# Two-layer float32 trunk on one core: four chained down accumulators, additions moved to the vector engine, transposes moved ahead

## The chip, the cores and the metric

One core of a Trainium2 chip runs the whole program in one launch. The core has a matrix engine (TensorE, PE in the profile, with PEld for its weight loads), a vector engine (VectorE, DVE), an activation engine (ScalarE, ACT), a general engine (GpSimd, POOL) and a queue that issues the DMAs (SyncE, SP). Each takes its own list of instructions in order, and waits on semaphores where it needs another's result. The matrix engine writes into PSUM (eight banks of 128 x 512 float32); the tiles that the other engines work on lie in SBUF. The metric is the device time of one execution in microseconds (us).

## The reference

The input is 1024 tokens of 1024 channels, and there are two layers. Every sub-layer is wrapped alike:

```
def sandwich(h, g_pre, g_post, fn):
    return x + rmsnorm(fn(rmsnorm(x, g_pre)), g_post)
def swiglu(h, w_gate, w_up, w_down):
    return (jax.nn.silu(h @ w_gate) * (h @ w_up)) @ w_down
```

Layer 0 mixes tokens by differential attention beside a convolution, layer 1 by an S5 state space beside latent attention. Each mixer ends in an output projection of 1024 x 1024; after each stands a SwiGLU of inner width 2816. All is float32, and accurate: each operand is split into a high part that the matrix engine takes in one pass and the remainder, and a product is three passes, high x high, high x low, low x high.

## The kernel before

**The pieces.** `mm3` (L114) issues the three passes. `wsplit` (L1116) makes a weight's high part on ACT and its low part on POOL (L1121). `to_T` transposes 128 rows through the PSUM tag `tr` (two one-bank slots). `sandwich` (L157) finishes 128 rows of a sub-layer: the row load, the sum of squares on ACT (L106), the reciprocal root on POOL (L97, L98), the scaling by root and gain on DVE (L164), the residual addition (L165) on the engine that the caller names, the store, and where a layer follows the next norm (L169).

**The SwiGLU** (`Ffn`) multiplies 2 x 2 blocks with seven products instead of eight (Strassen's scheme in Winograd's form). `x_sums` (L1094) prepares four input sums T1 to T4 and their splits; `up` writes seven forms of the hidden blocks to `h_s` in DRAM. `down` (L1227) goes through the eleven groups of the inner width one and then two at a time. A product (`prod`, L1258) of two groups is 24 matmuls: four blocks of 128 tokens, two groups, three passes; two token blocks share a PSUM tile of two banks (tag `big`, two slots). After half of them DVE adds the tile into an SBUF accumulator (L1229): seven accumulators, one for each product. The hidden blocks are split on ACT (L1248) and DVE (L1249), weight differences are formed on POOL (L1273, `g`). `top` does products 1, 5, 6, 2, 3, `low` does 7 and 4.

**The end of `down`.** For the last two steps (groups 7 to 10) `top` runs first for both. In the last `top` the seven accumulators are combined (`comb`, L1279 to L1282: two sums on POOL and five on DVE, each in two instructions of 128 x 1024). Then `end(0, ...)` runs `sandwich` for token blocks 0 to 3, and products 7 and 4 of the last four groups follow, 48 matmuls each, chained over these groups in PSUM, product 7 added into two accumulators, and `end(1, ...)` runs `sandwich` for blocks 4 to 7. In layer 0 (`end0`, L1412) the transposes of blocks 0 to 3 (`X1[0]`) are issued inside `end(1, ...)`, those of blocks 4 to 7 in `mla_in` (L803), between the first input projections of layer 1.

**Around the output projection.** `w_out_last` (L502) adds the second half of the projection to a stored part (L510), runs `sandwich` with POOL as the residual engine, and transposes the rows of two steps ago by `Ffn.to_T`, whose last difference (L1092) is on POOL. For each token block the projected input is split into one buffer `jt` (L484 on ACT, L485 on DVE).

**The order.** The program is written per tile; a planner (`schedule_with_timeline_sim=True`, L1547) puts the instructions of each engine in order by program order and modelled readiness. What runs is the fixed order it made.

Of the kernel before, what the change touches and what calls it, by code (L numbers as in the profile page):

```python
# [20 lines left out]
P = 128  # L21
# [14 lines left out]
class Trunk:  # L36
# [77 lines left out]
    def mm3(self, ps, a, b, first, last):  # L114
        mm = self.nc.tensor.matmul
# [41 lines left out]
    def sandwich(self, acc, tb, res, hout, gpost, gpre, r, eng):  # L157
# [6 lines left out]
        nc.vector.scalar_tensor_tensor(acc, acc, rs, v3(gpost), op0=ALU.mult, op1=ALU.mult)  # L164
        eng.tensor_tensor(r, r, acc, op=ALU.add)  # L165
# [336 lines left out]
    def w_out_last(self, Y, src, res, hout, gpost, gpre, G, pool, fin=None):  # L502
# [3 lines left out]
        for tb in range(8):  # L506
# [4 lines left out]
            self.sandwich(a, tb, res, hout, gpost, gpre, pool.tile([P, D], F32, tag="nr", name="nr", bufs=2), nc.gpsimd)  # L511
# [291 lines left out]
    def mla_in(self, X, pool, sp, accB, x2a):  # L803
# [59 lines left out]
        for hf in range(2):  # L863
# [21 lines left out]
            if hf == 0:  # L885
                x2a.close()
# [165 lines left out]
class Ffn:  # L1052
# [15 lines left out]
    def to_T(self, xn, tb):  # L1068
# [20 lines left out]
        if t:  # L1089
            v(f1[1], tr, f0[0], op=sub)  # L1090
            v(f1[0], tr, f1[0], op=sub)
            nc.gpsimd.tensor_tensor(f0[1], f0[1], f1[1], op=sub)  # L1092

    def x_sums(self, pool):  # L1094
# [11 lines left out]
        self.T3 = split(t("T3"), F1[:, 0], nc.gpsimd)  # L1106
        self.T4 = split(self.bx.tile([P, 4, 2, HALF], F32R, tag="f", name="T4"), F0[:, 1], nc.gpsimd)
# [119 lines left out]
    def down(self, end, ap, mid=None):  # L1227
        nc, K, v = self.nc, self.K, self.nc.vector
        add = lambda o, a, b: v.tensor_tensor(o, a, b, op=ALU.add)  # L1229
        hs = ExitStack()  # L1230
        hp = hs.enter_context(self.left("hp"))
        acc15 = ap.tile([P, 4, 2, HALF], F32, tag="a15", name="acc15")
        acc6 = ap.tile([P, 4, HALF], F32, tag="a6", name="acc6")
        acc23 = K.yp.tile([P, 4, 2, HALF], F32, tag="y", name="acc23")
        acc47 = K.yp.tile([P, 4, 2, HALF], F32, tag="y", name="acc47")
        a = {1: acc15[:, :, 0], 5: acc15[:, :, 1], 6: acc6, 2: acc23[:, :, 0], 3: acc23[:, :, 1], 4: acc47[:, :, 0], 7: acc47[:, :, 1]}

        half = lambda tag: hp.tile([P, 2, HALF], F32R, tag=tag, name=tag, bufs=3)
        spare = [half("hh"), half("hl")]
# [6 lines left out]
        def hsplit(r, n):  # L1246
            hi, lo = (spare.pop(0), spare.pop(0)) if spare else (half("hh"), half("hl"))
# [4 lines left out]
        def mm(ps, HW, tb, n):  # L1252
# [298 lines left out]
```

## Time and profile before

| what | value |
|---|---|
| median of three runs | 2391.94 us (2391.46 to 2400.63) |
| the profiled execution | 2392.32 us, span 2390.5 us, mean granted TensorE clock 0.955 |
| busy: PE, DVE, POOL, ACT | 2172.1, 1587.8, 1393.1, 952.2 us |
| layer 0: output projection; `up`; `down` | about 440 to 528; 528 to 980; 985 to 1230 us |
| layer 1: mixer; `up`; `down` | about 1245 to 1710; 1710 to 2135; 2136 to 2379 us |

Times in rows count from the start of the span. In a row of the timeline stand the start, the duration, the engine, the line, the operation, what it writes and reads, its shape, and in brackets how long its engine was idle before it and for whom it waited. The granted clock is 1 at 2.4 GHz and 0.5 at 1.2 GHz. A matmul's own duration (some 390 ns) overlaps the next one's; the distance of their starts is the rate.

### The profile page before, as it was taken

Reading aid. Unit: us, or ns where it says so; the run is one execution under the profiler, and the core shown is the slowest. Engines: PE = TensorE matmul, PEld = TensorE weight load, DVE = VectorE, ACT = ScalarE, POOL = GpSimd, SP = SyncE. Lnnn points to the kernel's source line nnn. Section 1 sums busy time; section 2 is a strip of 40 time slices with the busy share of each in tenths; the row PEclk is TensorE's granted clock in tenths of the full one; section 3 lists DMA queues with packets and bytes.
Section 4 is the critical chain, followed back from the end, with each engine's and each line's share of the span. In section 5 each row is a group of like instructions: output and inputs, shape, how many; then the busy total and the mean of one; then the engine's idle time right before and its main releaser. Section 6 shows DMA issues by size and latency. Waiting matters only on the chain. (4 is left out here: it accounts for less than half of the span.)

```text
span 2390.5 us, 27147 instructions
## 1 busy us (share of the span) xinstructions
PE 2172.1 (91%) x9684; PEld 1755.7 (73%) x9684; DVE 1587.8 (66%) x2091; ACT 952.2 (40%) x1419; POOL 1393.1 (58%) x790
## 2 busy tenths in 40 slices
PE   7999889876999999899768888998799999999995
PEld 5887677665888878688656776876688888877874
DVE  6869567679756865677883467756764444448778
ACT  5554555442222232433243346654522222234332
POOL 5997202264665556787843536423775656569786
PEclk9999899988999999999888999999899999999997
DMA  5134663342332333655453375324432323255543
GB/s 206 62 120 146 172 175 102 107 149 69 121 115 97 125 129 106 198 161 163 125 178 104 110 234 154 115 80 148 138 102 93 127 72 132 75 177 163 164 130 132
DMA packets 153735, 315.34 MB, mean 132 GB/s; under 512 B 20224, under 2 KB 43904, under 8 KB 153600
## 3 DMA queue, kind: packets, MB, share of 16 engines
q1 hardware_dynamic: 153600, 313.60, 40.8%
q8 instruction: 77, 1.26, 0.2%
q14 instruction: 58, 0.48, 0.1%
HBM read 214.39 MB, written 96.01 MB: 130 GB/s over the span
## 5 line engine op out<-in xcount | busy, mean ns | idle before, releaser
L1121 POOL TENSOR_TENSOR wl<-raw,wh 128x1024 fp32r<-128x1024 f32 (+1 forms) x238 | 607.4, 2556 | 335.9 <-ACT wh L1119 319.4
L1119 ACT CAST wh<-raw 128x1024 fp32r<-128x1024 f32 (+1 forms) x238 | 242.7, 1023 | 456.8 <-PE b L119 258.9
L118 PE MATMUL b<-T,wh 128*128 128x512 f32 x704 | 277.9, 396 | 16.3 <-DVE F L1170 13.0
L120 PE MATMUL b<-T,wl 128*128 128x512 f32 x704 | 277.4, 394 | 1.1 <-POOL wl L1121 1.1
L119 PE MATMUL b<-T,wh 128*128 128x512 f32 x704 | 277.7, 394 | 0.6 <-DVE T L1100 0.6
L118 PE MATMUL psd<-wh,hh 128*128 128x512 f32 x552 | 222.8, 404 | 37.7 <-DVE acc L1229 26.5
L118 PE MATMUL b<-B,wh 128*128 128x512 f32 x528 | 209.2, 397 | 21.2 <-DVE c L1161 17.6
L119 PE MATMUL psd<-wl,hh 128*128 128x512 f32 x552 | 219.9, 398 | 0.0
L120 PE MATMUL psd<-wh,hl 128*128 128x512 f32 x552 | 219.1, 398 | 0.0
L119 PE MATMUL b<-B,wh 128*128 128x512 f32 x528 | 208.2, 395 | 0.7 <-DVE B L1088 0.7
L120 PE MATMUL b<-B,wl 128*128 128x512 f32 x528 | 207.7, 395 | 0.8 <-POOL wl L1121 0.8
L1229 DVE TENSOR_TENSOR acc<-acc,psd 128x1024 f32<-128x1024 f32 x124 | 150.7, 1217 | 82.7 <-PE psd L120 82.6
L1170 DVE TENSOR_TENSOR p<-p,b 128x1024 f32<-128x1024 f32 (+1 forms) x88 | 83.4, 949 | 144.6 <-PE b L120 134.7
L1248 ACT CAST hh<-hr 128x1024 fp32r<-128x1024 f32 (+1 forms) x84 | 82.4, 981 | 240.0 <-PE psd L119 215.1
L118 PEld LDWEIGHTS b<-T,wh 128*128 128x128 f32 x704 | 133.1, 189 | 47.8 <-issue 13.6
L118 PEld LDWEIGHTS psd<-wh,hh 128*128 128x128 f32 x552 | 106.1, 192 | 70.1 <-issue 27.9
L91 POOL TENSOR_TENSOR wl<-raw,wh 128x1024 fp32r<-128x1024 f32 x48 | 121.6, 2546 | 61.6 <-ACT wh L89 61.4
L120 PEld LDWEIGHTS b<-T,wl 128*128 128x128 f32 x704 | 133.1, 189 | 31.8 <-POOL wl L1121 1.5
L119 PEld LDWEIGHTS b<-T,wh 128*128 128x128 f32 x704 | 133.3, 189 | 31.0 <-DVE T L1100 1.1
L1249 DVE TENSOR_TENSOR hl<-hr,hh 128x1024 fp32r<-128x1024 f32 (+1 forms) x84 | 145.7, 1738 | 11.9 <-ACT hh L1248 11.9
L1273 POOL TENSOR_TENSOR raw<-raw 128x1024 f32<-128x1024 f32 (+1 forms) x50 | 123.4, 2468 | 20.7 <-DMA raw<-in_l_dn_dram 18.3
L1171 DVE TENSOR_TENSOR raw<-raw 128x1024 f32<-128x1024 f32 x66 | 108.3, 1640 | 40.4 <-POOL wl L1121 39.1
(420 smaller groups left out, 5209.2 us busy)
## 6 DMA issues: line engine op xcount, KB each, us to landing
raw<-in_l_gu_dram SPq DMA_DIRECT2D x96, 512.0 KB, 3.5
hr<-l_h_s SPq DMA_DIRECT2D x70, 512.0 KB, 3.9
raw<-in_l_dn_dram SPq DMA_DIRECT2D x48, 512.0 KB, 3.8
l_h_s<-F SPq DMA_DIRECT2D x66, 256.0 KB, 2.2
raw<-in_w_in_dram SPq DMA_DIRECT2D x27, 512.0 KB, 4.0
l_h_s<-c SPq DMA_DIRECT2D x44, 256.0 KB, 2.0
l_h_s<-p SPq DMA_DIRECT2D x44, 256.0 KB, 2.4
raw<-in_l_w_out_dram SPq DMA_DIRECT2D x16, 512.0 KB, 4.1
```

The costliest lines, as they stand in the source:

```text
L91: nc.gpsimd.tensor_tensor(lo, raw, hi.bitcast(F32), op=ALU.subtract)
L118: mm(ps, ah, bh, start=first, stop=False)
L119: mm(ps, ah, bl, start=False, stop=False)
L120: mm(ps, al, bh, start=False, stop=last)
L1119: nc.scalar.copy(hi[:, 0:n], r[:, 0:n])
L1121: nc.gpsimd.tensor_tensor(lo[:, 0:n], r[:, 0:n], hi[:, 0:n].bitcast(F32), op=ALU.subtract)
L1170: add = lambda o, a, b: v.tensor_tensor(o, a, b, op=ALU.add)
L1171: sub = lambda o, a, b: v.tensor_tensor(o, a, b, op=ALU.subtract)
L1229: add = lambda o, a, b: v.tensor_tensor(o, a, b, op=ALU.add)
L1248: nc.scalar.copy(hi[:, 0:n], r[:, 0:n])
L1249: v.tensor_tensor(lo[:, 0:n], r[:, 0:n], hi[:, 0:n].bitcast(F32), op=ALU.subtract)
L1273: g = lambda o, x, y: nc.gpsimd.tensor_tensor(o[:, s], x[:, s], y[:, s], op=ALU.subtract)
```

## The change

- `down` keeps four accumulators. Products 1, 6, 5, 3 run in that order into the same two PSUM tiles without a restart, and after each the running sum is added into one accumulator (`wide`, 8 additions of 128 x 1024). Product 2 runs into four one-bank tiles (`slim`), and so does 7 with 4 chained on it: 12 additions of 128 x 512. The one-bank tiles are tags `tr`, `o` and `f`. All `comb` sums go. The differences for the last products 7 and 4 are formed on DVE (five in the tail); in the loop they stay on POOL.
- `sandwich` gets a second form (`m` given): the gain is multiplied while the root is computed, then one instruction scales and adds. The layer 1 `end1` uses it, on DVE.
- The residual addition of `w_out_last`, the last difference of `Ffn.to_T` and the low parts of T3 and T4 go from POOL to DVE.
- In layer 0 `end0` issues the transposes of blocks 0 to 3 right behind each block's `sandwich`, ahead of products 7 and 4. The tile for them is opened before `down`.

```diff
-            self.sandwich(a, tb, res, hout, gpost, gpre, pool.tile([P, D], F32, tag="nr", name="nr", bufs=2), nc.gpsimd)
+            self.sandwich(a, tb, res, hout, gpost, gpre, pool.tile([P, D], F32, tag="nr", name="nr", bufs=2), nc.vector)
...
+        if m is None:
+            nc.vector.scalar_tensor_tensor(acc, acc, rs, v3(gpost), op0=ALU.mult, op1=ALU.mult)
+            eng.tensor_tensor(r, r, acc, op=ALU.add)
+        else:
+            eng.tensor_tensor(v3(m), acc, v3(gpost), op=ALU.mult)
+            nc.vector.scalar_tensor_tensor(r, v3(m), rs, r, op0=ALU.mult, op1=ALU.add)
...
-            nc.gpsimd.tensor_tensor(f0[1], f0[1], f1[1], op=sub)
+            v(f0[1], f0[1], f1[1], op=sub)
...
-        self.T3 = split(t("T3"), F1[:, 0], nc.gpsimd)
-        self.T4 = split(self.bx.tile([P, 4, 2, HALF], F32R, tag="f", name="T4"), F0[:, 1], nc.gpsimd)
+        self.T3 = split(t("T3"), F1[:, 0], nc.vector)
+        self.T4 = split(self.bx.tile([P, 4, 2, HALF], F32R, tag="f", name="T4"), F0[:, 1], nc.vector)
...
+        def wide(pss, HW, n, k, start=False):
             for tp in range(2):
                 for b in range(2):
+                    mm(pss[tp][:, b], HW, 2 * tp + b, n, start)
+                drain(k, 2 * tp, 2 * tp + 2, pss[tp])
+
+        def slim(pss, HW, n, k, start=True):
+            for tb in range(4):
+                mm(pss[tb], HW, tb, n, start)
+                drain(k, tb, tb + 1, pss[tb])
+
+        def four():
+            return [*self.duo("tr", "psd"), *self.duo("o", "psd")]
+
+        def top(i, n):
+            pss = [K.pp.tile([P, 2, HALF], F32, tag="big", name="psd") for _ in range(2)]
+            B11 = ld(0, i, n)
+            wide(pss, [(hx(0, i, n), self.wsplit(B11, n))], n, (0, 0), True)
+            B12, T = ld(1, i, n), self.raw(None)
+            minus(nc.gpsimd, T, B12, B11, n)
+            W5 = self.wsplit(T, n)
+            B22 = ld(3, i, n)
+            minus(nc.gpsimd, T, B22, T, n)
+            wide(pss, [(hx(5, i, n), self.wsplit(T, n))], n, (1, 0))
+            wide(pss, [(hx(1, i, n), W5)], n, (1, 1))
+            wide(pss, [(hx(4, i, n), self.wsplit(B22, n))], n, (0, 1))
+            B21 = ld(2, i, n)
+            slim(four(), [(hx(2, i, n), self.wsplit(B21, n))], n, (0, 0))
             return B12, B21, B22, T
...
+        top(i1, n)
+        B = top(i2, n)
+        W7 = [w7(B, n, v)]
+        W4 = [w4(B, n, v)]
+        rows = lambda k: [ap.tile([P, D], F32, tag="r", name="r", bufs=4) for _ in range(k)]
+        end(0, out[0], rows(2), 0)
+        C12, C22 = ld(1, i1, n), ld(3, i1, n)
+        minus(v, C12, C22, C12, n)
+        W7.append(self.wsplit(C12, n))
+        q = four()
+        slim(q, [(hx(6, i, n), W) for i, W in zip((i2, i1), W7)], n, (1, 1))
+        end(0, out[0], rows(2), 2)
+        C11, C21 = ld(0, i1, n), ld(2, i1, n)
+        minus(v, C21, C21, C12, n)
+        minus(v, C21, C21, C11, n)
+        W4.append(self.wsplit(C21, n))
+        slim(q, [(hx(3, i, n), W) for i, W in zip((i2, i1), W4)], n, (1, 0), False)
         hs.close()
+        end(1, out[1], rows(4), 0)
...
-            for b in range(4):
-                K.to_T(st[0](b), X1[0], b)
+            X1.append(xb)
         for b, r in enumerate(res, b0):
             K.sandwich(row(b), 4 * hf + b, K.h1, K.h2, *st["g"], r, nc.vector)
+            if hf == 0:
+                K.to_T(row(b), X1[0], b)
```

`drain` adds a PSUM tile into its accumulator on DVE (the first time it copies, on ACT or DVE), `w7` and `w4` form and split a difference on the engine given.

## Rows read from the trace of the kernel before

**Rows 1.** Busy time by stage: window and length, PE, PEld, DVE, ACT, POOL, PEclk, DMA.
```profile
440.00:528.00 88.00, 79.65 (x357) 61.95 (x355) 55.02 (x64) 39.45 (x71) 42.98 (x44) 0.96 0.47 162
985.00:1177.00 192.00, 189.48 (x803) 152.70 (x804) 140.05 (x105) 78.15 (x82) 153.86 (x58) 0.98 0.55 173
1177.00:1275.00 98.00, 59.45 (x230) 45.51 (x229) 81.98 (x63) 35.31 (x57) 51.31 (x44) 0.76 0.44 147
2136.00:2326.50 190.50, 188.69 (x804) 151.01 (x804) 147.20 (x105) 78.72 (x82) 153.52 (x58) 0.99 0.54 172
2326.50:2379.20 52.70, 32.78 (x122) 25.05 (x120) 48.22 (x32) 11.91 (x18) 37.53 (x24) 0.84 0.35 120
488.00:491.20 3.20, 3.20 (x9) 2.55 (x8) 0.41 (x1) 0.89 (x2) 1.40 (x4) 0.52 0.30 120
```

**Rows 2.** Waits of PE, whole span: total us, times, longest us.
```profile
PE psd L118 <- DVE acc L1229: 26.5, 3, 12.3
...
PE ps L118 <- DVE acc L1229: 13.3, 6, 4.5
...
PE b L118 <- DVE F L1170: 13.0, 1, 13.0
...
PE psw L120 <- DVE jt L485: 10.4, 8, 1.7
```

**Rows 3.** Timeline, DVE and PE at the end of down; last row layer 1.
```profile
1175.21 3.40 DVE L1282 TENSOR_TENSOR acc<-acc,acc 128x1024 f32<-128x1024 f32 x1 [1.17 <-POOL acc L1282]
...
1181.82 6.63 DVE L1282 TENSOR_TENSOR acc<-acc,acc 128x1024 f32<-128x1024 f32 x2
...
1188.37 1.21 DVE L1229 TENSOR_TENSOR acc<-acc,psd 128x1024 f32<-128x1024 f32 x1
...
1189.72 0.76 PE L118 MATMUL psd<-wh,hh 128*128 128x512 f32 x1 [12.31 <-DVE acc L1229]
...
2339.08 0.77 PE L118 MATMUL psd<-wh,hh 128*128 128x512 f32 x1 [12.32 <-DVE acc L1229]
```

**Rows 4.** The combining sums on DVE, whole span: count, shortest/median/longest ns, first and last start.
```profile
L1282 DVE TENSOR_TENSOR acc<-acc,acc x20: 1207/2217/3402, 1170.7 to 2352.5; 128x1024 f32<-128x1024 f32 x20
```

**Rows 5.** Next norm of token blocks 4 and 7, timeline of DVE, layer 0.
```profile
1249.41 1.28 DVE L169 SCALAR_TENSOR_TENSOR acc<-acc,rstd,gpre 128x1024 f32<-128x1024 f32 x1 [0.99 <-POOL rstd L98]
...
1273.77 1.29 DVE L169 SCALAR_TENSOR_TENSOR acc<-acc,rstd,gpre 128x1024 f32<-128x1024 f32 x1 [1.27 <-POOL rstd L98]
```

**Rows 6.** The last two vector instructions of the kernel, timeline.
```profile
2383.82 1.28 DVE L164 SCALAR_TENSOR_TENSOR acc<-acc,rstd,gpost 128x1024 f32<-128x1024 f32 x1 [0.72 <-POOL rstd L98]
2385.13 1.23 DVE L165 TENSOR_TENSOR acc<-acc,acc 128x1024 f32<-128x1024 f32 x1
```

**Rows 7.** Timeline of POOL, DVE and PE in layer 0's output projection.
```profile
468.77 0.69 DVE L485 TENSOR_TENSOR jt<-yattn,jt 128x512 fp32r<-128x512 f32 x1
...
484.28 2.38 POOL L165 TENSOR_TENSOR nr<-nr,pa 128x1024 f32<-128x1024 f32 x1 [3.26 <-DVE pa L164]
...
484.72 2.49 DVE L485 TENSOR_TENSOR jt<-yattn,jt 128x512 fp32r<-128x512 f32 x1
...
487.26 0.51 PE L120 MATMUL psw<-wh,jt 128*128 128x512 f32 x1 [1.67 <-DVE jt L485]
```

**Rows 8.** Timeline, the input sums of layer 0's up, DVE and POOL.
```profile
554.27 2.27 DVE L1100 TENSOR_TENSOR T<-F,T 128x2048 fp32r<-128x2048 f32 x1
...
556.47 4.64 DVE L545 SCALAR_TENSOR_TENSOR xd<-xd,xd 128x8 f32<-128x8 f32 x1
...
563.42 4.59 POOL L1100 TENSOR_TENSOR T<-F,T 128x2048 fp32r<-128x2048 f32 x1
...
563.52 4.53 DVE L547 TENSOR_SCALAR xd<-xd 128x8 f32<-128x8 f32 x1
```

**Rows 9.** Groups in 1016 to 1177 us, by form: busy us, mean ns, idle before.
```profile
L1229 DVE TENSOR_TENSOR acc<-acc,psd 128x1024 f32<-128x1024 f32 x57 | 69.5, 1218 | 44.6 <-PE psd L120 44.5
...
L1121 POOL TENSOR_TENSOR wl<-raw,wh 128x1024 fp32r<-128x1024 f32 x29 | 82.5, 2848 | 23.7 <-ACT wh L1119 23.7
```

More of the change, by code (lines that the diff above doesn't have):

```diff
@@ L112, in bcast, with mm3 @@
         return t
-    def mm3(self, ps, a, b, first, last):
-        mm = self.nc.tensor.matmul
+    def mm3(self, ps, a, b, first, last, go=False):
+        mm = lambda *t, **k: self.nc.tensor.matmul(*t, skip_group_check=go, **k)
         ah, al = a
@@ L1225, in up, with down, ld, minus @@
         self.xs.close()
-    def down(self, end, ap, mid=None):
+    def down(self, end, ap):
         nc, K, v = self.nc, self.K, self.nc.vector
-        add = lambda o, a, b: v.tensor_tensor(o, a, b, op=ALU.add)
         hs = ExitStack()
         hp = hs.enter_context(self.left("hp"))
[L1232 to L1236, printed above, removed]
+        out = [K.yp.tile([P, 4, 2, HALF], F32, tag="y", name="acc") for _ in range(2)]
+        C = {(t, c): out[t][:, :, c] for t in range(2) for c in range(2)}
+        seen = set()
         half = lambda tag: hp.tile([P, 2, HALF], F32R, tag=tag, name=tag, bufs=3)
-        spare = [half("hh"), half("hl")]
+        def ld(blk, i, n):
+            return self.raw(self.dn[blk, i:i + n].rearrange("g p c -> p g c"), n)
+        def minus(eng, o, x, y, n):
+            eng.tensor_tensor(o[:, 0:n], x[:, 0:n], y[:, 0:n], op=ALU.subtract)
         def hraw(blk, i, n):
@@ L1255, in mm, with drain @@
                 for g in range(n):
-                    K.mm3(ps, (H[0][:, g, ts], H[1][:, g, ts]), (W[0][:, g], W[1][:, g]), i + g == 0, (i, g) == (len(HW) - 1, n - 1))
-        def prod(k, H, W, n, first):
+                    K.mm3(ps, (H[0][:, g, ts], H[1][:, g, ts]), (W[0][:, g], W[1][:, g]), start and i + g == 0, (i, g) == (len(HW) - 1, n - 1), True)
+        def drain(k, lo, hi, ps):
+            dst = C[k][:, lo:hi] if hi > lo + 1 else C[k][:, lo]
+            if (k, lo) not in seen:
+                seen.update((k, b) for b in range(lo, hi))
+                if lo < 2:
+                    nc.scalar.copy(dst, ps)
+                else:
+                    v.tensor_copy(dst, ps)
+            else:
+                v.tensor_tensor(dst, dst, ps, op=ALU.add)
@@ L1322, in down @@
-        B = top(i2, n, True)
-        free = [t[:, 2 * j:2 * j + 2] for t in (a[1], a[5], a[6], a[1]) for j in range(2)]
-        end(0, acc23, free[0:2], 0)
-        g, hx2, wx, ld = tools(i2, n)
-        _, hx1, _, ld1 = tools(i1, n)
-        B12, B21, B22, T = B
-        g(B12, B22, B12)
-        HW7 = [(hx2(6), wx(B12))]
-        g(B21, B21, T)
-        comb(v, 6, 6, 7)
-        comb(v, 7, 6, 5)
-        comb(v, 4, 4, 6)
-        end(0, acc23, free[2:4], 2)
-        C12, C22 = ld1(1), ld1(3)
@@ new lines, in w7, with w4 @@
+        def w7(B, n, eng):
+            minus(eng, B[0], B[2], B[0], n)
+            return self.wsplit(B[0], n)
+        def w4(B, n, eng):
+            minus(eng, B[1], B[1], B[3], n)
+            return self.wsplit(B[1], n)
+        for i, n in ((0, 1), *((i, 2) for i in range(1, NF // 2 - 4, 2))):
+            B = top(i, n)
+            q = four()
+            slim(q, [(hx(6, i, n), w7(B, n, nc.gpsimd))], n, (1, 1))
+            slim(q, [(hx(3, i, n), w4(B, n, nc.gpsimd))], n, (1, 0), False)
```

98 lines of the change are left out of this document (12 added, 86 removed).

## Prediction

> **What bounds the kernel now.** I read the busy time by stage first. In the body of both `down` stages PE works 189.48 of 192.00 us and 188.69 of 190.50 us at a granted clock of 0.98 and 0.99 [rows 1]. Nothing that leaves PE's own work alone can win there. It is otherwise at the two ends. From 1177 to 1275 us PE is busy 59.45 of 98.00 us, at a mean clock of 0.76; from 2326.5 to 2379.2 us 32.78 of 52.70 us, at 0.84 [rows 1]. DVE is busy 81.98 and 48.22 us there.
>
> The second view is the waits of PE. 26.5 us go to products that wait for the addition L1229, in three waits, and 13.3 us more to the last chained products [rows 2]. The third view, the timeline, shows why an addition of 1.21 us keeps PE waiting for 12.31 us in layer 0 and 12.32 us in layer 1: on DVE it stands behind combining sums, two of which take 6.63 us together [rows 3], where the shortest of the twenty takes 1.207 us [rows 4]. They are stretched: a DVE instruction that reads two SBUF tiles lasts until the POOL instruction beside it is over. The split L485 takes 0.69 us alone, and 2.49 us when it starts 0.44 us after a POOL addition of 2.38 us [rows 7]. The addition out of PSUM kept its 1.21 us [rows 3].
>
> So the ends are bound by what DVE and POOL can do one after the other, and the clock there falls to the lower of its two levels as well: the matmul at 1189.72 lasts 0.76 us [rows 3], against a spacing of 190.50 / 804 = 0.237 us in the body [rows 1].
>
> **The change part by part.** The sum is made against the profiled execution, 2392.32 us (1.8 us around its span of 2390.5); the median of three runs is 2391.94 us, the same within 0.4 us.
>
> *The body of `down`.* The matmuls are as many as before. A full round of two groups had 14 additions of 1.218 us [rows 9], now 8 of these and 12 of half the size; 0.69 us [rows 7] is my price for one. That is 12 x 0.69 - 6 x 1.218 = +1.0 us of DVE per round, beside 38 to 40 us of PE; DVE waited 44.6 us for PE in 161 us [rows 9], which hides it. Reuse of the two wide tiles is as tight as before: PE comes back to a tile after 12 matmuls (2.8 us). The one-bank tiles are four, with 3 x 6 matmuls (4.3 us) between. What is new is that product 6 comes second, so four POOL steps (difference, split, difference, split) must be done before it instead of two. One costs 2.85 us on average [rows 9], 11.4 us for four; the products in front (2, 7, 4 of the round before and 1) last 4 x 24 x 0.237 = 22.8 us. Hidden, with 11 us to spare. Lower bound -3 us (all the body's PE idle time), upper bound +61 us (a rival below); I take +2.
>
> *The end in layer 1.* The combining sums go: per layer ten on DVE and four on POOL. Product 7 is drained once. What stays on DVE and POOL from 2326.5 on, each at its unstretched length and in a row: four weight splits on POOL (2.4 each, as the POOL addition in rows 7: 9.6), four hidden splits and five differences on DVE (9 x 1.21 = 10.9), two instructions for each of the first four token blocks (1.21 + 1.28: 10.0), and four reciprocal roots (about 0.75 each, an estimate from the 0.72 us that DVE waits for one in rows 6 plus their start: 3). Sum 33.5 us. PE needs 120 matmuls x 0.237 = 28.4 us. So the larger, 33.5 us, plus 1 us for the first chain's start, stands against 52.7: -18.2 us. Behind the last product the chain of root, L164 and L165 loses L165, 1.23 us [rows 6], as the gain is multiplied while ACT and POOL make the root: -1.2. Together -19 us. Bounds: PE alone as limit, -24.3 - 1.2 = -25.5; nothing but the final addition, -1.
>
> *The end in layer 0.* The same sum with three DVE instructions a block (1.28 + 1.22 + 1.28, four blocks: 15.1) and two roots each (6): 9.6 + 10.9 + 15.1 + 6 = 41.6 us until product 4 is drained. Then come blocks 4 to 7. Before, their next norms ran from 1249.41 to 1273.77 us, four of them, 8.1 us apart [rows 5], behind the transposes of blocks 0 to 3 on the same engines. These transposes now lie between product 2 and the end of product 4, or just behind it, since two of their PSUM slots hold product 4's first sums: 8 halves of 0.69 us on DVE, 5.5 us, which DVE does from PSUM. I give 41.6 + 8 (the first block's chain) + 3 x 8.1 = 74 us against 98: -24 us. The moved step issues 32 transposes on PE, eight casts on ACT and eight remainders on DVE, no DMA and nothing on POOL; on PE, a transpose that waits for its block holds up the products behind it, which is rival 2. The row loads and stores of `sandwich` keep their place in SP's queue, and the four row tiles are free for blocks 4 to 7 once blocks 0 to 3 are stored, as the reused accumulators were. The tile that is opened earlier pushes the hidden blocks' tiles to other places, so their first loads may wait a little longer or shorter at the start of `down`; that is in the +2 above. Bounds: PE's own work is 59.45 x 0.76 = 45 us, so at best -53; at worst the sum stays DVE's 81.98 us less the ten combining sums at their shortest (12 us) plus five differences (6 us) and a start of 10 us, 86: -12. To lose there it needs the rival below.
>
> *Output projection.* Eight additions a layer go from POOL (2.38) to DVE (1.21). The seven to eight waits of 10.4 us for the split of `jt` [rows 2] come from the POOL addition [rows 7], and after some of them the clock is at the lower level for 3.2 us with 9 matmuls instead of 13 [rows 1]. If the split goes ahead of the addition it ends 1.8 us sooner and the wait is gone; if it goes behind, 0.6 us sooner. So between 8 x 0.6 = 5 and 10.4 + 3 = 13 us less over both layers, were PE's wait all. Against it, DVE has 8 x 1.21 = 9.7 us more per layer beside 55.02 of 88 us [rows 1], which can put off other drains: up to +5. I take -7.
>
> *Input sums.* T3 and T4 took POOL about 4.59 us each and DVE would take 2.27 [rows 8]. In layer 0 tiny DVE instructions stood behind them for 4.64 and 4.53 us [rows 8], in the queue that ends with the 13.0 us wait for L1170 [rows 2]. So DVE's queue is 9.2 - 4.5 = 4.6 us shorter; -4, bounds -9 (both hidden) and +5 (DVE longer and still stretched by other POOL work). In layer 1 PE has no such wait: 0. The difference L1092 (0.7 us on DVE) is hidden behind the same waits.
>
> Sum: 2 - 19 - 24 - 7 - 4 = -52; 2392.3 - 52 = **2340 us**.
>
> **The rivals.**
> 1. *The shared path fills up.* The ends stay bound by DVE and POOL because the vector engine's new differences collide with the weight splits and the early split of the next stage's weights (six of 2.4 us, 14 us) comes into the same row. For: ten sums at 2.2 us median [rows 4] show how stretched it runs. Against: POOL loses 4 x 2.4 + 5 x 2.4 us there. Layer 0 then saves 10, layer 1 9, projection and sums 3, body +2: **2372 us**. The Trainium skill (SBUF — State Buffer, Who interferes with whom) has the rule: GpSimd and a vector instruction with two SBUF inputs lock each other out of a shared port pair for the whole instruction. By that rule moving a difference to the vector engine frees nothing that runs beside it, only the difference of durations; the trace agrees (2.49 against 0.69 us). It would give this rival's time.
> 2. *The transposes don't lie under the products.* Their two PSUM slots are also product 7's and 4's. They then run behind product 4 as before, or hold up product 7 by a block's chain (8 to 10 us). Layer 0 saves 14 instead of 24: **2350 us**.
> 3. *PE becomes the bound at both ends*, with waits of a few us: -45 in layer 0, -23 in layer 1, -13, -8, 0 in the body: **2303 us**. For: PE's own work. Against: the sums of 33.5 and 41.6 us above.
> 4. *Slower: product 6 starves.* If the buffers for its two differences come free only with product 4, the four POOL steps (11.4 us) have only product 1 (5.7 us) in front: 5.7 us a round, five full rounds a layer, 57 us, and as much clock loss as makes 61. The gains fall to it: 2392 - 54 + 61 = **2399 us**. It decides from 5 us a round on. Against: weights have five slots and raw blocks five, and the slots that product 6 of the next round takes are freed by product 2 and the differences, before 7 and 4 run.
> 5. *The clock.* PE now returns to the same two PSUM tiles over four products; if its short pauses there put a tenth of the body at the lower level, that costs 0.1 x 382 = 38 us: **2378 us**. Against: the body cycled through the same two tiles before, at 0.98 and 0.99 [rows 1]. The Trainium skill (TensorE: Matmul & The Clock Gate, A second HAM failure mode: psum-queue depth-cycling) says that cycling through PSUM banks with small pauses makes the clock swing; the body here does not bear that out.
>
> **How the numbers follow.** Forecast 0.50, rivals 0.15, 0.12, 0.12, 0.07 and 0.04. What can be told from no change begins at 0.5%, 12 us. The forecast and rivals 2, 3 and most of 1 and 5 are faster by more: 0.88; the rest of 1, 4 and 5 within 0.5%: 0.06; rival 4: 0.06 slower. The range, 2304 to 2374 us, takes in most of rival 3 and of rival 1 and leaves out 4.
>
> **What would show it.** The two waits of 12.3 us are gone and no wait over 6 us stands at either end; the stretch from the last top's end to the first `psc` is near 74 us in layer 0, and 34 us to PE's end in layer 1; one DVE instruction behind the last root; `jt` waits under 5 us in total; the body still at 0.98 and 0.237 us a matmul. It is wrong if PE waits for L1121 or L1273 in every round, or if new waits for weights at the ends sum to over 15 us a layer.

## The result, and the profile after

The changed kernel takes **2334.07 us** (median of four runs, 2331.67 to 2341.0) against 2391.70 us of the kernel before beside it: a ratio of 0.9754, 95% interval 0.9727 to 0.9782. Forecast were 2340 us. The profiled execution took 2335.67 us, its span is 2333.9 us. PE's busy time went from 2172.1 to 2155.4 us, POOL's from 1393.1 to 1275.4; DVE's stayed (1583.1 us).

The first view answers [rows 1]: the output projection of layer 0, then each `down`, cut in two at the end of its 804th matmul, first layer 0, then layer 1. In the new order these 804 take in the first four products of the last `top`; its fifth, 24 matmuls, already belongs to the end. Where the prediction says "the last top's end", this cut is meant.

```profile
440.00:528.00 88.00, 78.25 (x367) 61.24 (x366) 67.66 (x80) 43.85 (x76) 27.62 (x39) 0.99 0.49 172
969.60:1167.80 198.20, 190.08 (x804) 152.63 (x805) 160.18 (x139) 74.66 (x78) 145.24 (x51) 0.98 0.51 162
1167.80:1235.60 67.80, 52.64 (x211) 41.28 (x210) 52.34 (x44) 29.84 (x47) 34.61 (x34) 0.85 0.47 154
2094.50:2292.20 197.70, 190.35 (x803) 153.20 (x804) 155.57 (x140) 74.79 (x78) 143.37 (x51) 0.98 0.50 162
2292.20:2324.20 32.00, 29.55 (x122) 23.52 (x121) 27.71 (x28) 11.64 (x18) 15.23 (x15) 0.95 0.44 147
```

Both ends are much shorter: 67.8 us where the kernel before needs 96.1 from its 804th matmul to the first `psc`, and 32.0 where [rows 1] has 52.7. PE is busy for 92% of the end in layer 1, so hardly anything but PE is left there. But the two bodies, forecast at +2 us in all, are *longer*: 198.2 and 197.7 us, with PE's busy time nearly what it was.

The second view, PE's longest waits over the whole span (total, times, longest), answers [rows 2].

```profile
PE psd L115 <- ACT hh L1252: 20.3, 2, 12.3
PE psd L115 <- DVE acc L1271: 17.7, 10, 3.0
PE tr L181 <- DVE xt L184: 11.2, 5, 4.7
PE b L115 <- DVE c L1163: 10.4, 3, 5.1
```

The two waits of 12.3 us for an addition behind combining sums are gone. The wait for `F` is 3.1 us instead of 13.0, and those for DVE's half of `jt` come to 0.5 us instead of 10.4; for ACT's half PE waits 6.9 us in the two projections (5.6 before). What leads now are the two waits for the first hidden block at the start of `down`, 12.3 and 8.0 us (5.4 and 4.0 before), and ten short ones for drains. One more row of the kernel before, its second longest, which [rows 2] leaves out and the prediction doesn't use, has come down too:

```profile
PE b L118 <- DVE c L1161: 17.6, 2, 9.1
```

These are waits behind each output projection, 8.5 us in layer 0 and 9.1 in layer 1, for `c`, the additions on DVE that drain the first products of `up`. In the changed kernel they are 4.0 and 6.4 us.

The span cut at PE's own landmarks (first or last matmul of a product, read from both timelines):

| stretch | before | after | difference |
|---|---|---|---|
| start to layer 0's last output projection | 447.1 | 446.5 | -0.6 |
| layer 0: output projection and input sums, to the first product with T1 | 107.4 | 95.7 | -11.7 |
| `up`, to its last product | 424.9 | 414.7 | -10.2 |
| to the first `down` product | 5.8 | 12.7 | +7.0 |
| `down`, to the 804th matmul's end | 192.0 | 198.2 | +6.2 |
| to layer 1's first `psc` | 96.1 | 67.8 | -28.3 |
| layer 1: mixer and output projection | 418.5 | 414.0 | -4.5 |
| to the first product with T1 | 42.2 | 39.2 | -3.0 |
| `up` | 398.0 | 397.4 | -0.6 |
| to the first `down` product | 4.4 | 8.4 | +4.0 |
| `down`, to the 804th matmul's end | 190.2 | 197.7 | +7.5 |
| to PE's end | 52.6 | 32.0 | -20.6 |
| to the end of the span | 11.3 | 9.7 | -1.6 |

The sum is -56.4 us of the spans' -56.6. So the total came near the forecast because misses of both signs met: some 25 us lost at the start of `down` and in its last `top`s, where 2 were forecast, and some 15 us more won ahead of it, 7 at the ends and 4 in layer 1's mixer stretch. The experiments went after these.

### The profile page after: what moved, and what is told of

The parts are those of the page before. It is cut to its first block, busy times and chain, and to the rows that moved or that the text cites. A ratio compares the mean times of both kernels' runs of the same rounds, so it can differ in the third digit from the quotient of the medians.

```text
span 2333.9 us, 27188 instructions
## 1 busy us (share of the span) xinstructions
PE 2155.4 (92%) x9684; PEld 1744.8 (75%) x9684; DVE 1583.1 (68%) x2175; ACT 945.6 (41%) x1413; POOL 1275.4 (55%) x740
## 3 DMA queue, kind: packets, MB, share of 16 engines
q1 hardware_dynamic: 150528, 313.60, 41.6%
## 4 chain that ended last, share of the span: by engine, by line
PE 68%; DVE 13%; DMA 6%; issue 5%; POOL 4%; ACT 3%; SPq 1%; POOLq 0%; DVEq 0%; ACTq 0%
PE b L115 30%; PE psd L115 13%; PE psw L115 6%; PE psc L115 5%; PE psq L115 3%; PE po L115 2%; PE pss L1038 2%; POOL wl L1123 2%; PE trp L365 1%; DVE hl L1253 1%; DVE acc L1271 1%; DMA bm<-k_s 1%; PE psv L115 1%; PE psu L115 1%; DMA hr<-l_h_s 1%
## 5 line engine op out<-in xcount | busy, mean ns | idle before, releaser
L115 PE MATMUL b<-T,wh 128*128 128x512 f32 x1408 | 438.6, 393 | 3.1 <-DVE F L1172 3.1
L115 PE MATMUL b<-B,wh 128*128 128x512 f32 x1056 | 335.2, 398 | 13.8 <-DVE c L1163 10.4
L115 PE MATMUL psd<-wh,hh 128*128 128x512 f32 x616 | 248.3, 404 | 42.3 <-ACT hh L1252 20.3
L115 PEld LDWEIGHTS b<-B,wh 128*128 128x128 f32 x1056 | 201.6, 191 | 60.3 <-ACT B L1089 7.0
L115 PE MATMUL psd<-wl,hh 128*128 128x512 f32 x616 | 245.9, 400 | 0.0
L115 PE MATMUL psd<-wh,hl 128*128 128x512 f32 x616 | 234.5, 400 | 2.2 <-DVE hl L1253 2.2
L1271 DVE TENSOR_TENSOR acc<-acc,psd 128x512 f32<-128x512 f32 (+1 forms) x208 | 178.1, 884 | 73.1 <-PE psd L115 73.1
L115 PE MATMUL psw<-wh,jt 128*128 128x512 f32 x512 | 175.5, 408 | 17.1 <-ACT jt L488 9.6
L115 PEld LDWEIGHTS b<-T,wl 128*128 128x128 f32 x704 | 132.1, 188 | 33.8 <-POOL wl L1123 3.9
L115 PEld LDWEIGHTS psd<-wh,hl 128*128 128x128 f32 x616 | 118.6, 193 | 30.9 <-DVE hl L1253 3.9
L115 PEld LDWEIGHTS psd<-wl,hh 128*128 128x128 f32 x616 | 118.8, 193 | 26.0
```

Of the source, the lines that this page charges most:

```text
L115: mm = lambda *t, **k: self.nc.tensor.matmul(*t, skip_group_check=go, **k)
L1271: v.tensor_tensor(dst, dst, ps, op=ALU.add)
```

## The experiments

Each kernel is the changed one with the edit shown; "the changed kernel" is 2334.1 us, and 2334.7 us where it ran again in the last group (its ratio there 0.9765). The kernel before beside these groups had 2392.6, 2388.9 and 2389.2 us.

**1. Everything moved to the vector engine goes back (e1_pool_back).**

```diff
-            self.sandwich(a, ..., name="nr", bufs=2), nc.vector)
+            self.sandwich(a, ..., name="nr", bufs=2), nc.gpsimd)
-            v(f0[1], f0[1], f1[1], op=sub)
+            nc.gpsimd.tensor_tensor(f0[1], f0[1], f1[1], op=sub)
-        self.T3 = split(..., nc.vector);  self.T4 = split(..., nc.vector)
+        self.T3 = split(..., nc.gpsimd);  self.T4 = split(..., nc.gpsimd)
```

> Undoes one part alone in the changed kernel: the output projection's residual addition, the splits of T3 and T4 and the last difference of the feed-forward transposes go back from the vector engine to GpSimd. Theory A (these moves gave what the segments of the two traces show, 5.9 and 5.2 us in the two output projections and 16.0 and 3.6 us between them and the first down product): 2334 + 31 = about 2365 us, with the 13 us wait for F of layer 0's up stage back. Theory B (the prediction's own terms, 7 and 4): 2334 + 11 = 2345 us. Theory C (the 10.2 us saved late in layer 0's up stage belong to the written order of the s5 preparation and not to these moves): about 2355 us, and the wait for F stays at 3 us.

Measured: 2363.76 us, ratio 0.9876 (0.9846 to 0.9907). Theory A: these four small moves are worth 30 us, half of the whole change. The 13 us wait is back. This is DVE in front of it, and PE's wait, in this kernel:

```profile
553.20 4.62 DVE L549 SCALAR_TENSOR_TENSOR xd<-xd,xd 128x8 f32<-128x8 f32 x1
...
557.86 2.33 DVE L550 SCALAR_TENSOR_TENSOR xd<-xd,xd 128x8 f32<-128x8 f32 x1
...
560.23 4.52 DVE L551 TENSOR_SCALAR xd<-xd 128x8 f32<-128x8 f32 x1
...
564.98 0.97 DVE L553 SCALAR_TENSOR_TENSOR xd<-xd,xd 128x8 f32<-128x8 f32 x5
...
570.62 2.31 DVE L553 SCALAR_TENSOR_TENSOR xr<-xr,xr 128x8 f32<-128x8 f32 x1
...
577.20 1.21 DVE L1172 TENSOR_TENSOR p<-p,b 128x1024 f32<-128x1024 f32 x1
...
581.09 1.19 PE L115 MATMUL b<-T,wh 128*128 128x512 f32 x2 [12.99 <-DVE F L1172]
```

The same in the changed kernel:

```profile
556.75 1.21 DVE L1172 TENSOR_TENSOR p<-p,b 128x1024 f32<-128x1024 f32 x1
...
562.13 0.69 PE L115 MATMUL b<-T,wh 128*128 128x512 f32 x2 [3.12 <-DVE F L1172]
```

GpSimd's last split (T4) lasts from 560.12 to 564.71 us. By then PE is done with the products that pair 0's sum `p` needs (in run 9, where `p` waits for them, this is 11.2 us after the first product with T1, which makes 562.5 here), and it stops at 568.1. Yet DVE gets to `p` at 577.20: from 564.7 us on 98 tiny instructions of layer 1's state-space preparation stand in front of it in DVE's queue. Of the 102 smallest of these (128x8 to 128x32) 100 stand ahead of `p` here, as in the kernel before, and 25 in the changed kernel. Two readings are left. One is the order: they needn't stand there. The other is the duration: beside GpSimd's work, from 553.2 to 564.7 us, three of them alone hold DVE for 11.5 us, and a fourth for 2.31 us later, where one usually takes 0.16. Run 9 tests the order.

**2. The transposes of blocks 0 to 3 late again (e2_late_transposes).**

```diff
+            X1.append(K.x_tiles(x2a.enter_context(left("x2a", 2))))   # opened in end0 again
+            for b in range(4):
+                K.to_T(st[0](b), X1[0], b)
-            if hf == 0:
-                K.to_T(row(b), X1[0], b)
-    X1.append(K.x_tiles(x2a.enter_context(left("x2a", 2))))
```

> Undoes the early transposes alone: layer 1's first input tile is opened, and blocks 0 to 3 are transposed, after layer 0's last product, as in the kernel before; the four chained accumulators stay. Theory A (the transposes under the products are worth their time at the end of layer 0): the stretch from layer 0's 804th down matmul to layer 1's first psc grows from 67.7 to 78 us, and the first down product of layer 0 comes 3 us sooner because the loads of h no longer wait for the last store: about 2341 us. Rival B (lying between product 7's blocks they hold the PE for 9 us, so that they gain nothing): the stretch stays within 3 us, 2331 to 2334 us.

Measured: 2330.71 us, ratio 0.9735 (0.9709 to 0.9761): no slower. On the stretch to `psc` rival B is right, 66.0 against 67.8 us; of theory A only the start holds, where the first `down` product comes 3.1 us sooner. Layer 0's whole way from the first `down` product to `psc` is 266.3 us with the transposes late and 266.0 with them early. So this part of the change, the earlier transposes, gives nothing at the end and costs 3 us at the start.

**3. The tail's weight differences on GpSimd (e3_tail_pool).**

```diff
-        W7 = [w7(B, n, v)]
-        W4 = [w4(B, n, v)]
+        W7 = [w7(B, n, nc.gpsimd)]
+        W4 = [w4(B, n, nc.gpsimd)]
...
-        minus(v, C12, C22, C12, n)      # and both differences of C21
+        minus(nc.gpsimd, C12, C22, C12, n)
```

> Moves the five weight differences of the last two index pairs' low products back from the vector engine to GpSimd, as they were before. Theory A (on the vector engine they stand ahead of the drains and cost the 6.0 and 7.5 us that the last tops lose against the kernel before): 804 matmuls of down take 193 instead of 198 us in both layers, total 2334 - 10 = 2324 us. Rival B (GpSimd is the later engine there, each difference costs 2.8 us ahead of a split on the same queue, and the locked port holds the drains as well): the loss moves to waits for wl and the total is 2334 to 2342 us.

Measured: 2325.63 us, ratio 0.9719 (0.9687 to 0.9752). Theory A. In the timeline of the changed kernel this is layer 1's last `top`, DVE, POOL and PE:

```profile
2240.84 6.71 POOL L1123 TENSOR_TENSOR wl<-raw,wh 128x1024 fp32r<-128x1024 f32 x2
...
2242.24 3.08 DVE L1242 TENSOR_TENSOR raw<-raw 128x1024 f32<-128x1024 f32 x1 [0.27 <-DMA raw<-in_l_dn_dram]
...
2245.24 1.21 DVE L1271 TENSOR_TENSOR acc<-acc,psd 128x1024 f32<-128x1024 f32 x1
...
2246.51 0.80 PE L115 MATMUL psd<-wh,hh 128*128 128x512 f32 x1 [2.50 <-DVE acc L1271]
...
2281.14 1.21 DVE L1242 TENSOR_TENSOR raw<-raw 128x1024 f32<-128x1024 f32 x1
```

The difference takes 3.08 us, where one with POOL idle takes 1.21 (last row): POOL's first split ends at 2244.2 us, and the difference 1.1 us later. The drain, which stands behind it in DVE's queue, waits as long, and PE for the drain. PE's next matmuls are at the lower level of the clock (granted 0.51 from 2246.5 to 2249 us). With the differences on POOL, body and end of layer 1's `down` (columns as above):

```profile
2087.60:2279.60 192.00, 187.28 (x802) 151.47 (x803) 147.56 (x134) 74.86 (x79) 153.36 (x55) 0.99 0.53 166
2279.60:2311.40 31.80, 28.65 (x124) 22.62 (x122) 29.77 (x29) 11.96 (x18) 17.88 (x16) 1.00 0.43 148
```

192.0 us instead of 197.7, and the end is no longer for it. In layer 0 the body falls by 2.2 us, to 196.0, but there the changed kernel's own second profile (run 12) is 2.7 us longer than its first. The two last `top`s alone (216 matmuls up to the cut) tell more: they grew from 49.8 to 57.5 us in layer 0 (58.2 in run 12) and from 49.6 to 57.1 in layer 1, and are 53.1 and 51.9 us here. So 2 to 3 us of the growth stay in each layer, and no run shows their cause.

**4. The sandwich's first row loads held back (e4_late_rows).** Eight one-column copies that read the last `top`'s B22 are written into the row tiles ahead of their loads.

```diff
+            if touch:
+                for r in rs:
+                    v.tensor_copy(r[:, 0:1], B[2][:, 0, 0:1])
```

> In both down stages the first four residual-row loads of the sandwich get a one-column vector copy ahead of them that reads the last top's B22, so that the load queue can't send them at the start of down (eight tiny instructions more). Theory A (four 512 KB row loads ahead of the loads of h cost the first down product its time): layer 1's wait for hh falls from 8.0 to about 4 us and layer 0's from 12.3 to 8 or less, total 2334 - 7 = 2327 us. Theory B (in layer 0 the loads of h wait for the last store because the early-opened input tile moved their buffers): layer 1 gains 4, layer 0 nothing, 2330 us. Rival C (the loads of h are late for another reason): 2334 us.

Measured: 2335.78 us, ratio 0.9757 (0.9729 to 0.9785): no gain that the runs can tell. In the trace B is right on both starts. The load queue and PE at the start of layer 1's `down`, first the changed kernel, then this one:

```profile
2081.51 1.37 SPq L162 DMA_DIRECT2D r<-h  x3
2083.54 0.58 SPq L162 DMA_DIRECT2D r<-h  x1
2085.55 0.44 SPq L1246 DMA_DIRECT2D hr<-l_h_s  x1
...
2094.54 0.79 PE L115 MATMUL psd<-wh,hh 128*128 128x512 f32 x1 [8.00 <-ACT hh L1252]
```

```profile
2087.13 0.42 SPq L1246 DMA_DIRECT2D hr<-l_h_s  x1
...
2091.79 0.79 PE L115 MATMUL psd<-wh,hh 128*128 128x512 f32 x1 [3.68 <-ACT hh L1252]
```

Without four loads of 512 KB ahead of it PE's wait is 3.7 instead of 8.0 us. Layer 0's start gained 1.0 us, and its stretch from the first `down` product to `psc` is 2.4 us longer (1.4 of that also separate the changed kernel's own two profiles); the start of the span, ahead of any change, was 3.3 us later in this execution.

**5. The residual additions alone back on GpSimd (e5_proj_back).** The first edit of run 1 alone.

> Undoes the output projection's additions alone (one argument: the residual addition goes back to GpSimd); T3, T4 and the last transpose difference stay on the vector engine. Together they cost 30 us when all went back. Theory A (each part gives what its own segments show): the two output projections grow by 5 us each, 2334 + 10 = 2344 us, and the wait for F in layer 0 stays at 3 us. Theory B (the additions also push the input sums later, since the last rows' transposes and sums are queued behind them): 2334 + 20 = 2354 us, with layer 0's way from the last output projection product to the first up product back at 39 us. Theory C (the additions give nothing by themselves, the splits all): 2334 us.

Measured: 2349.07 us, ratio 0.983 (0.9803 to 0.9858): between A and B. B's place is right: in layer 0 the stretch of output projection and input sums is 106.3 us again (95.7 in the changed kernel), 3.7 us of it in the projection and 6.9 behind it, and `up` keeps its 413.9. In layer 1 it costs nothing that stands out: 297.8 us from the mixer's `psgl` to the first product with T1, against 298.7. PE's waits in layer 0's projection, and the POOL addition that makes the first of them:

```profile
485.40 2.37 POOL L166 TENSOR_TENSOR nr<-nr,pa 128x1024 f32<-128x1024 f32 x1 [3.27 <-DVE pa L165]
```

```profile
488.38 0.73 PE L115 MATMUL psw<-wh,jt 128*128 128x512 f32 x2 [1.66 <-DVE jt L489]
...
498.02 0.73 PE L115 MATMUL psw<-wh,jt 128*128 128x512 f32 x2 [1.40 <-DVE jt L489]
...
536.28 1.19 PE L115 MATMUL b<-B,wh 128*128 128x512 f32 x2 [8.74 <-DVE c L1163]
```

The waits for `jt` are those forecast. The third row is not: behind the projection PE waits 8.7 us for `c` where the changed kernel waits 4.0. That this is because each row's addition, and with it the last rows' transposes, comes later is argued.

**6. The early transposes through the wide PSUM tiles (e6_big_tr).**

```diff
+            pair = self.pp.tile([P, 2, 4, P], F32, tag="big", name="tr")
...
-            tr = self.pp.tile([P, 4, P], F32, tag="tr", name="tr")
+            tr = pair[:, q] if big else self.pp.tile([P, 4, P], F32, tag="tr", name="tr")
...
-                K.to_T(row(b), X1[0], b)
+                K.to_T(row(b), X1[0], b, True)
```

> Blocks 0 to 3 of layer 1's input are transposed through the two wide PSUM tiles, which are free after the last top, instead of the two tiles that the low products' accumulators also use; nothing else is changed. Theory A (in the changed kernel the products of 7 wait for the transposes' tiles and the transposes for the norm, 9 us of gaps, and that is why the early transposes gained nothing): from the 804th down matmul to psc 67.7 falls to about 59 us, 2334 - 9 = 2325 us. Rival B (the norm chain of blocks 4 to 7 and their transposes set the end, whatever is done early): 66 to 68 us, total 2332 to 2336 us.

Measured: 2334.12 us, ratio 0.9772 (0.9751 to 0.9792): no change. Rival B. The last `down` product comes 9 us sooner after the first (234.9 against 244.1 us), and the transposes wait instead, for the norm (L173) and for their own evacuation:

```profile
1211.70 0.63 PE L183 MATMUL tr<-ident,acc 128*128 128x128 f32 x4 [2.62 <-DVE acc L173]
...
1221.40 1.29 DVE L173 SCALAR_TENSOR_TENSOR acc<-r,rstd,gpre 128x1024 f32<-128x1024 f32 x1 [1.27 <-POOL rstd L98]
...
1222.83 1.09 PE L183 MATMUL tr<-ident,acc 128*128 128x128 f32 x4 [5.42 <-DVE acc L173]
```

The DVE row is the norm of block 3, the last that the first `psc` needs. The same norm in the changed kernel and in run 2:

```profile
1205.50 1.28 DVE L173 SCALAR_TENSOR_TENSOR acc<-r,rstd,gpre 128x1024 f32<-128x1024 f32 x1 [1.59 <-POOL rstd L98]
```

```profile
1215.90 1.28 DVE L173 SCALAR_TENSOR_TENSOR acc<-r,rstd,gpre 128x1024 f32<-128x1024 f32 x1 [0.99 <-POOL rstd L98]
```

`psc` starts 66 us after the 804th matmul, as with late transposes. Three orders of transposes, slots shared or not, give 66 to 68 us. Counted from the 804th matmul, block 3's norm comes at 46 us in run 2 and at 47 us here. In the changed kernel it comes at 38 us, but products and transposes have shared the slots, and the last product isn't over before 46 us. From whichever of the two ends last it is 19 to 22 us to `psc`. PE's waits on the way, nearly all for DVE's drains, norms and transposes' remainders, sum to 15 or 16 us in each of the three.

**7. The new `down` alone (e7_down_alone).** Runs 1 and 2 together and no `m` form: all that is left of the change is the chained accumulators with their order of products.

> The chained accumulators alone: the kernel before with the down stage's new order of products and its two accumulator tiles, and nothing else of the change (additions, splits and last difference on GpSimd, transposes late, no m form at layer 1's end). Theory A (the parts add up: 30 from the moves to the vector engine, minus 3 from the late transposes, 1 from the m form): 2334 + 30 - 3 + 1 = 2362 us, 30 below before. Theory B (the parts need each other, since GpSimd's share of the work comes back in the tail): 2370 us or more.

Measured: 2362.51 us, ratio 0.9885 (0.9854 to 0.9916). Theory A: the two halves of the change add up, within the scatter of this kernel's four runs (2354.75 to 2370.20 us). It also shows the `m` form by itself, as the last rows of DVE in this kernel and in the changed one:

```profile
2350.55 1.28 DVE L165 SCALAR_TENSOR_TENSOR acc<-acc,rstd,gpost 128x1024 f32<-128x1024 f32 x1 [0.72 <-POOL rstd L98]
2351.75 2.35 DVE L166 TENSOR_TENSOR r<-r,acc 128x1024 f32<-128x1024 f32 x2
```

```profile
2328.88 1.29 DVE L169 SCALAR_TENSOR_TENSOR r<-m,rstd,r 128x1024 f32<-128x1024 f32 x1 [0.72 <-POOL rstd L98]
```

From the last matmul's start to the end of the span it is 11.6 us without and 10.0 with it.

**8. Late transposes, tail on GpSimd, late row loads (e8_late_all).** The edits of runs 2, 3 and 4.

> Three edits of the earlier runs together on the changed kernel: transposes late, the tail's weight differences on GpSimd, the first four row loads held back. Theory A (they add up: -3, -8, -4 and in layer 0 another -3, because with the input tile opened late and no row loads ahead the loads of h are sent between the last stores as in the kernel before): 2334 - 18 = 2316 us. Theory B (tail differences and late transposes share one cure, the vector engine's load at the end, and the row loads gain nothing in time): 2324 us.

Measured: 2326.92 us, ratio 0.9739 (0.972 to 0.9757): below the forecast of A. Both starts are as A says: PE's first waits for `hh` are 4.3 us in layer 0 and 3.1 us from the last `up` product to the first of `down` in layer 1. But in layer 0 the gain comes back 35 us later as a wait that the changed kernel does not have:

```profile
999.48 0.74 PE L115 MATMUL psd<-wh,hh 128*128 128x512 f32 x2 [1.86 <-ACT wh L1121]
1005.00 0.80 PE L115 MATMUL psd<-wl,hh 128*128 128x512 f32 x1 [4.79 <-POOL wl L1123]
```

POOL had waited 4.5 us for a weight's load (`raw`) until 984.07 us, and from there had eight differences and splits in a row, to 1007 us. With that the first full round takes 47 us instead of 39.

**9. Run 1 with the state-space preparation held back (e9_s5_late).** Its first table is written once from pair 2's result, so none of its instructions can stand ahead of that.

```diff
+        v.tensor_copy(lam[:, 0, 0:1], self.gate)
         nc.sync.dma_start(lam, io["s5_lam"])
...
         both(p1, 2)
+        K.gate = p1[:, 0, 0:1]
```

> The first run's kernel (everything moved to the vector engine put back on GpSimd) with one more edit: the state-space preparation that layer 0's up stage carries along can't start until pair 2 is done (its first table is written once from that pair's result). Theory A (the 13 us wait for F in layer 0 is the written order: some 120 small preparation instructions stand on the vector engine ahead of pair 0's sums, put there because GpSimd's two splits come late): the wait falls to 4 us or less and from the first to the last up product takes 415 instead of 425 us, 2364 - 10 = 2354 us. Theory B (GpSimd's splits themselves hold F that long): the wait stays at 13 us, 2364 us.

Measured: 2353.06 us, ratio 0.9837 (0.9813 to 0.9862). Theory A. GpSimd does its splits as slowly as in run 1, yet pair 0's sum starts at 564.15 us and PE doesn't wait for `F` there; `up` takes 411.2 us. So the place in the queue is enough to take the wait away. With it goes the stretching of the tiny instructions that stood there, and no run keeps their place and takes GpSimd's splits from beside them: whether the durations alone would have been enough stays open.

```profile
560.96 4.61 POOL L1103 TENSOR_TENSOR T<-F,T 128x2048 fp32r<-128x2048 f32 x1
```

```profile
564.15 1.22 DVE L1173 TENSOR_TENSOR p<-p,b 128x1024 f32<-128x1024 f32 x1 [10.03 <-PE b L115]
```

**10 to 12. The best of it, one more form, and the changed kernel again.** Run 10 has late transposes, the tail on GpSimd, and late row loads in layer 1 only. Run 11 adds the `m` form for blocks 4 to 7 of layer 0. Run 12 is the changed kernel.

```diff
-    def down(self, end, ap):
+    def down(self, end, ap, hold=False):      # hold: run 4's copies; set in layer 1
...
+            K.sandwich(..., f0.tile([P, D], F32, tag="m", name="m", bufs=2) if hf else None)   # run 11
```

> The changed kernel with transposes late (as in the second run), the tail's weight differences on GpSimd (third run) and the row loads held back in layer 1 alone (the fourth run's edit, without layer 0, where the eighth run lost 7 us to late weights). Theory A (the parts add up in the traces: 3 at the start of layer 0's down, 4 at layer 1's, 8 in the tails): 2334 - 15 = 2319 us, with no wait for wl over 2 us at the start of layer 0's down. Theory B (medians hold only half of what the traces add up to): 2324 to 2327 us.

> The tenth run's kernel with the product by the gain ahead of the root in layer 0's end too (blocks 4 to 7), as layer 1's end has it. Theory A (the vector engine is busy for four fifths of layer 0's end, and each block's chain loses one vector instruction behind the root, 1.3 us for each of the last two blocks): 2 to 4 us below the tenth run. Rival B (the vector engine's instructions are as many, so its queue is as long): within 1 us. Rival C (the gain's product now stands ahead of the transposes' splits and they come later): 2 us above.

> The changed kernel without any edit, beside the other three on the same chip: 2334 us, within 3 us, against which the tenth and eleventh runs are read.

Measured: **2319.59 us**, ratio 0.9703 (0.968 to 0.9726), for run 10; 2328.73 us, 0.9743 (0.9719 to 0.9766), for run 11; 2334.69 us, 0.9765 (0.9742 to 0.9788), for run 12. Run 10 is A's number and beats both kernels: 15 us below the changed one beside it. No wait for `wl` of 1 us or more stands at layer 0's start. Its two stages of layer 1's `down`:

```profile
2078.10:2271.10 193.00, 188.19 (x804) 151.27 (x805) 151.05 (x138) 74.89 (x78) 160.03 (x58) 0.99 0.53 178
2271.10:2302.60 31.50, 28.30 (x122) 22.36 (x120) 29.74 (x28) 11.96 (x18) 17.56 (x16) 1.00 0.45 150
```

Run 11 is rival C, at a larger price. The norms of blocks 6 and 7 do come sooner: the last instruction L173 ahead of layer 1 starts at 1234.98 us, 268.6 us after the first `down` product, against 270.4 in run 10. But that of block 3, which the first `psc` needs, comes 2.7 us later, and the planner's new order puts 20 of the 32 transposes of blocks 4 to 7 ahead of the first `psc`, where run 10 has 8. From the first `down` product to `psc` it is 271.3 us, 9 more than run 10's 262.2, and the next stage keeps the loss.

## Why the prediction was right, and where not

**The ends, -24 and -19: the cause was right, the sums behind them were not.** From the 804th matmul to `psc` it is 67.8 us (74 forecast), to PE's end in layer 1 32.0 (34). No wait over 6 us stands there, one DVE instruction is behind the last root, and the `m` form gives 1.6 us (1.2 forecast). That the old `down` made the ends long is shown by run 7, where the new one alone brings them to 65.7 and 33.8 us. But neither sum describes what was left.

- In layer 1 it had DVE and POOL work in a row for 33.5 us. They are busy 27.7 and 15.2 us of the 32.0, and PE 29.6: the five differences on DVE, 6 us of that sum, had run ahead of the cut, and PE is the bound, as rival 3 has it.
- In layer 0 the sum let `psc` wait for the norms of blocks 4 to 7. It needs only blocks 0 to 3, and starts at 1235.59 us, ahead of the norms of blocks 6 and 7 (1240.37 and 1247.58 us). Until the last product it took 46 us, where 41.6 were forecast, and then 21 instead of 32 us to `psc`. This landmark also moves with the order, since 24 transposes of blocks 4 to 7 stand ahead of it in the kernel before and 8 in the changed one; measured to the mixer's first `psgl` the end gained 25.0 us.

That both totals came out so near is partly luck.

**"These transposes now lie between product 2 and the end of product 4": half true, and worth nothing.** Rival 2 had the shared slots right: in the changed kernel blocks 0 and 1 sit in PE's queue between blocks of product 7 and hold them, and blocks 2 and 3 run behind product 4.

```profile
1193.47 1.94 PE L181 MATMUL tr<-ident,acc 128*128 128x128 f32 x8 [4.09 <-DVE acc L173]
1197.24 0.79 PE L115 MATMUL psd<-wh,hh 128*128 128x512 f32 x1 [1.83 <-DVE xt L184]
```

Its price (10 us) was wrong: runs 2 and 6 show the same 66 to 68 us wherever the transposes lie. The -24 was right with the wrong share in it; all of it comes from the new `down`.

**The body, +2: the step that failed.** It took in the start of `down` and the last `top`s and measured +24.7 us over both layers (7.0 + 6.2 + 4.0 + 7.5). The rounds between are as forecast: the last two full ones take some 38.5 us each before and after, the body's clock is 0.98, and PE waited for no weight split and no difference there, so rivals 4 and 5 fall. The two omissions:

- *"The row loads and stores of `sandwich` keep their place in SP's queue"* was wrong. The reused accumulators kept the row loads late; the new row tiles are free from the start, and the planner sent four loads ahead of the first hidden blocks. In layer 1 that is the whole 4.0 us (run 4). In layer 0 it comes on top of the earlier-opened tile. With it all loads of the hidden blocks are issued behind the last store of `up`, without it between the stores; that their buffers' new places are the reason is argued, not tried. PE's wait is 12.3 us with both, 11.3 without the rows (run 4), 9.3 without the tile (run 2), 4.3 without either (run 8).
- *"Five differences on DVE"* were priced at 1.21 us and put into the end alone. All five of each layer run in the last `top`s instead, ahead of drains, and last up to 3.41 us beside POOL's splits. Moving them back gave 8 us by the medians and the 5.7 us of layer 1's body (run 3). Rival 1 had named the collision and placed it at the ends, where it cost little. The Trainium skill (SBUF — State Buffer, Who interferes with whom) says that a vector instruction with two SBUF inputs and GpSimd's reads exclude each other for the whole instruction. The trace agrees: 3.08 us beside a split, 1.21 us alone.

**Output projection, -7, and input sums, -4: too small, and one read only in part.** The additions are worth 15 us by the medians (run 5), 10.6 by the trace, of which 3.7 lie in the projection, where the `jt` waits were reckoned with, and 6.9 behind it, 4.7 of them in the wait for `c`. The prediction left these out, though the 17.6 us for `c` stood second among PE's waits. The splits and the last difference are worth the other 15: 10.2 in layer 0's `up`, and about 5 in layer 1 behind the mixer, where 0 was forecast. In layer 0 the prediction read the 13.0 us wait as tiny instructions stretched by POOL (9.2 us of them). Run 9 takes the wait away with the splits left on POOL, by the tiny instructions' place in the queue alone. In the changed kernel both are different: the planner puts pair 0 ahead of most of them, and the splits of T3 and T4 no longer stand beside them. So the stretching that the prediction counted isn't refuted as a part of the wait; the order, which it took as given, is what it overlooked.

So two errors of opposite sign met. The new `down` alone gave 26 us (run 7: 2388.9 to 2362.5) where 2 - 19 - 24 = -41 were forecast (that sum includes the early transposes and the `m` form, which run 7 leaves out; by runs 2 and 7 they cost 3 us and give 1.6), and the moves to the vector engine 30 where 11 were.

**Open:** the mixer stretch of layer 1, -4.5 us in the table, has no part assigned to it. Kernels with the very same code there (runs 2, 3, 4, 6, 8, 10 to 12) spread from 407.9 to 412.3 us over it, the longest of them run 12, which is the changed kernel itself; its first profile has 414.0. The 5 us of the input sums in layer 1 are read from landmarks of runs 1, 5, 7 and 9 alone; no run took the splits and the last difference apart. That run 11's loss comes from its order is argued from the rows, not tried. Of the last `top`s' loss 2 to 3 us a layer remain with the differences back on GpSimd, without a cause. And no run parts the tiny instructions' place from their stretching.

## What to carry to other kernels

When a tile gets its own buffer instead of a reused one, look at which loads were held back by the reuse: they will now be issued as early as the order lets them, ahead of the loads that the next stage needs first. Before moving an operation to a less busy engine, read what stands behind it in that engine's queue at that place; a 1 us instruction in front of a PSUM drain can be paid by PE (2.5 us in run 3), and a move can change the order of a long run of small ones, not only durations. A total that comes out right proves none of its terms: undo the parts one at a time.

## What the runs showed that was not expected

- A few moved instructions make the planner rewrite the order of a whole stage: run 11 changed one form and lost 9 us by layer 1's first `psc`, although the last two blocks were ready 2.6 and 1.8 us sooner.
- GpSimd holds up even the smallest vector instructions: a 128x8 instruction that usually takes 0.16 us took 4.52 us beside a 4.59 us split of GpSimd's (run 1).
- The stretch ahead of every change, 446 us in the changed kernel, lay between 445.0 and 452.6 us in the thirteen profiled executions made of the changed kernel and its variants. A single profile can't carry differences of a few us in the total. Stretches between landmarks carry more, but not all of it: the changed kernel's two profiles agree within 0.1 us on layer 1's body and differ by 2.7 us on layer 0's.
